# A decode step on one core: the order of narrow attention scores, of their transposes, and of the first and last steps

## The chip, the cores and the metric

The kernel runs on one core of one Trainium2 chip. The metric is device time in microseconds (us) of one execution. Before the change the median of three runs is 603.91 us (602.45 to 604.02).

The engines are named as in the profile: PE is the tensor engine (its weight loads are listed apart, as PEld), DVE the vector engine, ACT the scalar engine with its function tables, POOL the general engine, and SP the one that issues most of the transfers.

## The reference

One decoder layer and a final norm, for a prompt of 256 tokens and for 8 sequences of 4 new tokens each with 2048 cached tokens:

```
h = rms_norm(x, g);  z = h @ w_in          # one projection for all head groups
y_a = silu(c_g) * short_conv(...)          # gated convolution
k_cmp = compress(kv_all[k], ...)           # 64 cached keys pooled to one
s = q @ k_cmp;  p = softmax(s)             # compressed scores, 32 blocks
blocks = top_k(sum of p over heads, forced blocks)
o_sel = softmax(q_rot @ k_sel[blocks]) @ v_sel[blocks]
o_win = softmax(q_rot @ k_win) @ v_win     # the last 512 keys
y_b = silu(n_g) * (g0*o_cmp + g1*o_sel + g2*o_win)
y_m = silu(m_g) * attend(m_q, mem_k, mem_v)   # 256 memory tokens
y = rms_norm(x + concat(y_a, y_b, y_m) @ w_out, final_g)
```

`rms_norm` divides by the root of the mean square. The memory keys and values of the prompt come from `rms_norm(mem_prompt) @ w_mem_kv`. The new cache rows are returned as well.

## The kernel before, in words

The main stream of PE is the projection. Tokens (288 of them, prompt and sample together) are the moving columns, and the weights come as 128 x 1024 halves, each of eight 128 x 128 tiles. Both sides are split into a high and a low part, so that a half is 24 products: high by high, high by low, low by high. `w_load` brings a half from memory, `w_hi` (ACT) rounds it, and `w_lo` (DVE) makes the rest, `wl`. The first four halves, for the memory keys of the prompt, are multiplied without a split, by `first_tiles` (line 290): two output tiles `zf` of 16 steps (k tiles) each. Its input is scaled by `m_scale` (four DVE operations of 256 elements and one ACT copy, the high part) and `m_low` makes the low part for the tiles that follow. Two tiles of PSUM take the outputs in turn; `mem_tile` evicts each on ACT.

All other work is spread between these products by a planner that runs when the program is built. Small generators yield between their steps. `chunk` (line 162) moves the plan's clock `now` by one and lets each waiting generator take a step; it is called twice for a half, every 12 products. The planner keeps its own estimates of the engines' clocks in `at`: `matmul` (line 113) adds 0.2 us for each change between products with 32 weight columns and others, `until` yields while PE's clock is behind another engine's. The result is one fixed order of instructions on each engine.

The work for the 8 sequences goes in two halves of four sequences (`hf` 0 and 1). `stage_stream` (line 821) takes staged pieces of the caches in a fixed order. Cached keys are multiplied with the queries by `scores` (line 494): 16 products of 32 weight columns, four bands of 32 rows that share one PSUM tile, which ACT copies into 512 columns of the score tile `S`. The cached values (`values`, line 625) and the sample's memory keys and values (`memk_use`, `memv_use`) are visits of the same narrow form. `dec_cmp` (line 443) projects the pooled keys and values, multiplies the queries with the compressed keys (tile `sc`, eight products of 32 columns, narrow as well), takes their softmax, and turns the 16 largest blocks into an additive mask `madd`. `dec_softmax` (line 554) adds the mask, 64 keys a block, and takes the softmax. `weights` (line 614) transposes four times 128 columns of `S`, into `pv`: a value tile holds four successive keys in each partition, so transpose n takes every fourth column, n, n + 4, and so on.

`rsqrt` (line 200) makes 1/root in steps: a `Sqrt` on ACT, a reciprocal on DVE, one Newton step on DVE. It is used for the memory tokens and the input rows near the start, and at the end for three groups of rows (two of 128 prompt tokens, one of the sample, called r0, r1 and r2 here). At the end the last 512 output columns are computed with tokens as rows. `squares` sums them, `factors` calls `rsqrt`, `spread_rows` (line 1716) brings the factors of the rows across the partitions with a product (tile `rb`), `scale_tiles` multiplies the 12 column tiles with them, four at a time, and sends them out. `decode_rows` are the sample's products for these columns, 16 steps, and between step `SPREAD_AT` (line 75) and the next stands the spread of r1. `busy` issues products whose result isn't used.

Of the kernel before, what the change touches and what calls it, by code (L numbers as in the profile page):

```python
# [12 lines left out]
AF = mybir.ActivationFunctionType  # L13
ALU = mybir.AluOpType
AX = mybir.AxisListType
# [58 lines left out]
TAIL_BUSY = (4, 6)  # L74
SPREAD_AT = 13
DT = 12
# [4 lines left out]
def decode_step(ctx, tc, xT, xN, xD, xL, fgl, memT, cst, w_in, w_mem, w_out, w_bg, pt, ptv, ckc, ckk, ckv, wk, wv, mk, mv,  # L81
# [59 lines left out]
    vec, act = Timed(nc.vector, VEC, 0.03, 0.0011), Timed(nc.scalar, ACT, 0.16, 0.00083)  # L141

    def behind(i, j):

        at[i] = max(at[i], at[j])
# [48 lines left out]
    def C(name):  # L194
        o, w = _COFF[name]
        return c[:, o:o + w]
# [3 lines left out]
    def rsqrt(r, ssq, rest=None, room=None):  # L200

        v, t = room or (small(3, "yv", 1)[:, :r.shape[1]], small(3, "yt", 1)[:, :r.shape[1]])
        if rest is not None:
            act.activation(r, ssq, AF.Sqrt, scale=1.0 / D, bias=rest[0])
            vec.scalar_tensor_tensor(v, ssq, -0.5 / D, rest[1], op0=ALU.mult, op1=ALU.add)
            vec.reciprocal(r, r)
            vec.scalar_tensor_tensor(t, r, r, v, op0=ALU.mult, op1=ALU.mult)
            vec.scalar_tensor_tensor(r, t, 1.5, r, op0=ALU.add, op1=ALU.mult)
            return
        act.activation(r, ssq, AF.Sqrt, scale=1.0 / D, bias=C("eps"))  # L210
        vec.tensor_scalar(v, ssq, 1.0 / D, EPS, op0=ALU.mult, op1=ALU.add)
        vec.reciprocal(r, r)
        vec.tensor_tensor(t, r, r, op=ALU.mult)
        vec.scalar_tensor_tensor(t, t, -0.5, v, op0=ALU.mult, op1=ALU.mult)
        vec.scalar_tensor_tensor(r, t, 1.5, r, op0=ALU.add, op1=ALU.mult)
# [74 lines left out]
    def first_tiles():  # L290
# [7 lines left out]

        for k0 in (0, 2, 4, 6):
            for i in range(2):  # L300
                part(i, k0, 2)
            if k0 == 2:
                first_loads(0)
                m_scale(8)
                m_low(0)
            elif k0 == 4:
                m_scale(12)
                m_low(4)
            elif k0 == 6:
# [12 lines left out]
        for s in (2, 3):  # L322
            w_hi(s + 2)
            w_lo(s + 1)
            part(s - 2, 8, 4)
            chunk()
            part(s - 2, 12, 4)
            w_load(s + WR)
            first_loads(s)
            nhalf[0] = s + 1  # L330
            yield z[s - 2]
# [111 lines left out]
    def dec_cmp(hf):  # L443
# [12 lines left out]
        act.activation(Vc, t[:, :256], AF.Copy)  # L456
        yield from until(VEC)
        S = env["S", hf]
        s = pss.tile([128, 512], F32, name=f"sc{hf}", tag="s")
# [34 lines left out]
    def scores(hf, o, t, keys):  # L494

        s = pss.tile([128, 512], F32, name=f"sk{hf}", tag="s")
        keys = [keys(x) for x in t]
        for c0 in range(2):
            for g in range(2):
                for b in range(4):  # L500
                    matmul(s[32 * b:32 * b + 32, c0 * 256:c0 * 256 + 256], qcols(0, 4 * hf + b, g), keys[2 * c0 + b // 2](b % 2, g),
                           start=(g == 0), stop=(g == 1), skip_group_check=True)
        act.activation(env["S", hf][:, o:o + 512], s, AF.Copy)

# [23 lines left out]
    def wink_use(hf, t):  # L528
# [17 lines left out]
        vec.tensor_tensor(S[:, C_NW:C_NW + 32], s[:, 32:64], nmask, op=ALU.add)  # L546
        w = S[:, C_NW - 4:C_NW]
        behind(VEC, ACT)
# [5 lines left out]
    def dec_softmax(hf):  # L554
# [4 lines left out]
        for i in range(4):  # L559
            sel = S[:, C_SEL + i * 512:C_SEL + (i + 1) * 512].rearrange("p (n j) -> p n j", j=64)  # L560
            vec.tensor_tensor(sel, sel, env["madd", hf][:, i * 8:i * 8 + 8].unsqueeze(2).to_broadcast([128, 8, 64]), op=ALU.add)
            vec.tensor_reduce(mx[:, i:i + 1], sel, axis=AX.XY, op=ALU.max)
            yield 1
# [50 lines left out]
    def weights(hf, q):  # L614

        o = C_WIN if q == 0 else C_SEL + (q - 1) * 512
        w = env["S", hf][:, o:o + 512]
        parts = w.rearrange("p (r c) -> p c r", c=4)
        t = ptr.tile([128, 512], F32, name=f"pv{hf}", tag="t")
# [5 lines left out]
    def values(hf, i, t):  # L625

        o, PT = env["o"], env["PT", hf, i]
        t = [x.rearrange("p (n c) -> p n c", n=4) for x in t]
# [49 lines left out]
    def memk_use(j, t):  # L678
        if j == 0:
            assert "o" not in env  # L680
            env["o"] = 1
            env["mo"] = pos.tile([128, 512], F32, name="smd", tag="o")
        s = env["mo"]
        for h, x in enumerate(t):
            tv = x.rearrange("p (c s) -> p c s", c=4)
# [35 lines left out]
    def memv_use(j, t):  # L721
        if j == 0:
# [4 lines left out]
            env["mo"] = pos.tile([128, 512], F32, name="omd", tag="o")  # L727
        o = env["mo"]
        PTm = Sm.rearrange("p b s -> p (b s)")
        for k, x in enumerate(t):  # L730
# [181 lines left out]
    nc.gpsimd.memset(z0, 0.0)  # L912
    act.activation(small(1, "mx1"), z0[:, 0:1], AF.Sqrt)
    ps = pss.tile([128, 512], F32, name="zeros", tag="s")
# [690 lines left out]
    def second_pass(n, z):  # L1605
# [10 lines left out]
        if n == DT - 3:  # L1616
            act.activation(small(1, "mx1"), C("eps"), AF.Sqrt)

# [97 lines left out]
    def spread_rows(g, r):  # L1716
        n, k = (128, 128) if g < 2 else (32, 32)
        matmul(rb[:, g * 128:g * 128 + n], r[:k].to_broadcast([k, 128]), ident[:k, :n], start=True, stop=True)

# [58 lines left out]
    matmul(ssq[:, 3:4], sel, sums2[:, 2:3], start=True, stop=True)  # L1778
    scale_tiles(1, 4, 8, nc.sync)
    gains(2)  # L1780
    scale_tiles(1, 8, 12, nc.sync)
    r2 = factors(2, ssq[:, 3:4])
# [139 lines left out]
```

## Time and profile before

| | |
|---|---|
| median of three runs | 603.91 us |
| the profiled execution | 602.7 us |
| its span, first to last instruction | 600.9 us |
| PE busy | 593.2 us, 4827 instructions |
| DVE busy | 457.2 us, 739 instructions |
| ACT busy | 303.5 us, 541 instructions |
| POOL busy | 204.3 us, 281 instructions |
| mean granted PE clock | 0.999 |
| moved by DMA | 190.84 MB |

The lines of the profile that follow name an engine, an operation and the tiles (`out<-in`) with their shape and count. In a timeline the first column is the start in us from the span's start, the second the duration of the group. A group's idle time stands in square brackets, with what ended it. Products are pipelined: one starts before the one ahead of it has ended, so the distance from start to start is what a product costs, and not its duration. Nearly all operations have the line of a helper, so the tiles' names tell them apart.

### The profile page before, as it was taken

The page shows a single profiled execution, that of the slowest core. Times are in us where ns is not written, and L with a number is a line of the kernel's source. Part 1 is how long each engine was busy: PE and PEld are TensorE (multiplying, and loading weights), DVE is VectorE, ACT ScalarE, POOL GpSimd, SP SyncE. Part 2 cuts the span into 40 slices and gives each one's busy share as a digit, 9 for nine tenths or more (in the row PEclk, how much of TensorE's full clock was granted, in tenths as well). Part 3 has the DMA queues.
Part 4 walks back from the last instruction along what each step waited for, and adds up shares of the span by engine and source line. Part 5 has one row for each costly group of instructions (what it writes and reads, how often), then busy time and mean ns, then how long its engine had stood idle before and what let it go on. Part 6 is the DMA issues. An engine that isn't in the chain of part 4 may idle for free.

```text
span 600.9 us, 13265 instructions
## 1 busy us (share of the span) xinstructions
PE 593.2 (99%) x4827; PEld 544.4 (91%) x4827; DVE 457.2 (76%) x739; ACT 303.5 (51%) x541; POOL 204.3 (34%) x281
## 2 busy tenths in 40 slices
PE   8999999999999999999999999999999999999997
PEld 6987999989999999989999899999998998979996
DVE  3999799988596679978897879887768742357665
ACT  4887446444456434434455444555553453435653
POOL 2013554434245333414554544223111334422200
PEclk9999999999999999999999999999999999999999
DMA  8999888999989998987799898898989999979834
GB/s 306 416 429 399 272 306 319 325 306 375 326 269 370 380 415 308 342 327 248 265 331 326 286 368 289 276 339 290 317 311 331 363 333 318 326 253 365 280 143 159
DMA packets 76194, 190.84 MB, mean 318 GB/s; under 512 B 8864, under 2 KB 26432, under 8 KB 75872
## 3 DMA queue, kind: packets, MB, share of 16 engines
q0 software_dynamic: 26016, 100.48, 47.4%
q1 hardware_dynamic: 49104, 88.12, 40.8%
q10 hardware_dynamic: 1008, 1.38, 0.7%
q8 instruction: 38, 0.62, 0.4%
q14 instruction: 28, 0.23, 0.1%
HBM read 184.74 MB, written 13.60 MB: 330 GB/s over the span
## 4 chain that ended last, share of the span: by engine, by line
PE 87%; DVE 7%; DMA 3%; issue 1%; ACT 1%; ACTq 0%; SPq 0%; DVEq 0%
PE z L121 61%; PE zr L121 4%; PE zv L121 4%; PE od L121 3%; PE sk L121 3%; DMA mraw<-memT 2%; DVE pooled L138 2%; PE s L121 2%; DVE wl L138 2%; PE acc L121 2%; PE pv L126 1%; PE pt L126 1%; PE zf L121 1%; DMA st<-ckc 1%; PE om L121 1%
## 5 line engine op out<-in xcount | busy, mean ns | idle before, releaser
L121 PE MATMUL z<-x,wh 128*128 128x288 f32 x1664 | 248.2, 298 | 0.4 <-ACT wh L138 0.4
L121 PEld LDWEIGHTS z<-x,wh 128*128 128x128 f32 x1664 | 227.4, 188 | 7.0 <-issue 4.2
L138 DVE TENSOR_TENSOR wl<-w,wh 128x1024 fp32r<-128x1024 f32 x147 | 181.7, 1239 | 63.7 <-PE z L121 33.2
L138 ACT ACTIVATE wh<-w 128x1024 fp32r<-128x1024 f32 x148 | 154.3, 1052 | 20.0 <-PE z L121 13.1
L121 PE MATMUL z<-x,wl 128*128 128x288 f32 x832 | 127.0, 295 | 0.6 <-DVE wl L138 0.6
L121 PEld LDWEIGHTS z<-x,wl 128*128 128x128 f32 x832 | 115.3, 188 | 1.5 <-DVE wl L138 1.4
L415 POOL TENSOR_TENSOR st<-st,cst 128x512 f32<-128x512 f32 x56 | 62.3, 1112 | 109.5 <-issue 55.5
L230 POOL DMA_DIRECT2D w<-w_in x104 | 58.4, 562 | 111.9 <-DVE wl L138 79.3
L138 DVE TENSOR_REDUCE pooled<-st 128x16 f32<-128x1024 f32 x56 | 67.7, 1210 | 2.2 <-POOL st L415 2.1
L138 DVE TENSOR_TENSOR st<-st,cst 128x512 f32<-128x512 f32 x56 | 39.1, 697 | 8.0 <-DMA st<-ckc 7.9
L230 POOL DMA_DIRECT2D w<-w_out x32 | 17.6, 551 | 67.3 <-DVE wl L138 42.1
L642 POOL DMA_INDIRECT st<-ckv,rows_v x29 | 31.5, 1087 | 22.0 <-PE od L121 13.0
L138 ACT ACTIVATE P<-P,nm 128x128 f32<-128x128 f32 (+1 forms) x32 | 14.2, 444 | 30.3 <-DVE nm L138 30.3
L121 PE MATMUL z<-y,wh 128*128 128x288 f32 x192 | 27.2, 294 | 0.0
L121 PEld LDWEIGHTS z<-y,wh 128*128 128x128 f32 x192 | 26.0, 188 | 0.1
L121 PE MATMUL sk<-st,qz 128*32 128x256 f32 x288 | 19.7, 382 | 0.0
L121 PE MATMUL od<-st,S 128*32 128x256 f32 x288 | 18.9, 382 | 0.0
L138 ACT ACTIVATE se<-z 128x288 f32<-128x288 f32 x16 | 6.4, 401 | 22.0 <-PE z L121 22.0
L121 PE MATMUL zf<-mixed,w 128*128 128x256 f32 x64 | 15.3, 394 | 1.0 <-DVE mixed L138 0.7
L121 PEld LDWEIGHTS zf<-mixed,w 128*128 128x128 f32 x64 | 12.0, 194 | 4.7 <-DVE mixed L138 2.4
L121 PE MATMUL z<-y1b,wh 128*128 128x288 f32 x84 | 15.3, 296 | 0.0
L138 ACT ACTIVATE P<-P,sm 128x128 f32<-128x128 f32 (+1 forms) x32 | 11.9, 444 | 6.4 <-DVE sm L138 6.2
(356 smaller groups left out, 813.2 us busy)
## 6 DMA issues: line engine op xcount, KB each, us to landing
w<-w_in POOLq DMA_DIRECT2D x104, 512.0 KB, 6.3
st<-ckc SPq DMA_DIRECT2D x112, 256.0 KB, 5.9
w<-w_out POOLq DMA_DIRECT2D x32, 512.0 KB, 6.2
st<-ckk SPq DMA_DIRECT2D x112, 128.0 KB, 4.9
w<-w_mem SPq DMA_DIRECT2D x12, 512.0 KB, 7.4
o_wk<-wk POOLq DMA_DIRECT2D x8, 512.0 KB, 7.5
o_wv<-wv POOLq DMA_DIRECT2D x8, 512.0 KB, 7.3
qk<-ckc SPq DMA_DIRECT2D x16, 256.0 KB, 6.2
```

The source lines that it names most:

```text
L121: nc.tensor.matmul(out, a, b, **kw)
L126: nc.tensor.transpose(out, a, b)
L138: return getattr(self.engine, name)(*args, **kw)
L230: (nc.gpsimd if s >= ON_SYNC else nc.sync).dma_start(raws[s], wsrc[s])
L415: done.append(eng.tensor_tensor(tm[:, :, kv], tm[:, :, kv], acmp[:, kv].unsqueeze(1).unsqueeze(1).to_broadcast([128, 2, 4, 64]), op=ALU.mu ...
L642: nc.gpsimd.indirect_dma_start(t, None, ckv, bass.IndirectOffsetOnAxis(ap=rows_v[:, j * 4 + b:j * 4 + b + 1], axis=0))
```

## The change

- `dec_cmp` waits, for up to six chunks, until a narrow visit has been planned in the same chunk, and puts the compressed scores behind it (`beside`). The narrow visits (`scores`, `values`, `memk_use`, `memv_use`) note the chunk in `narrow`.
- `scores` writes its 512 columns as four groups of 128: key 4r + c of the piece goes to column 128c + r. `weights` then transposes adjacent columns. The mask of the window, the addition of `madd` and the maximum follow the new order.
- `rsqrt` uses one ACT function for 1/root, without the reciprocal; the two calls that prepare ACT's table use it as well.
- `first_tiles` takes the two tiles in turn up to k tile 12, and two of its side steps are reordered.
- At the end: `SPREAD_AT` 11 for 13; the spread of the sample's factors uses all 128 rows; one `scale_tiles` goes ahead of `gains(2)`.

```diff
-SPREAD_AT = 13
+SPREAD_AT = 11
...
+    narrow = [-1]
+    def beside(n):
+        for _ in range(n):
+            if narrow[0] == now[0]:
+                return
+            yield 1
...
-            act.activation(r, ssq, AF.Sqrt, scale=1.0 / D, bias=rest[0])
+            act.activation(r, ssq, AF.Abs_reciprocal_sqrt, scale=1.0 / D, bias=rest[0])
             vec.scalar_tensor_tensor(v, ssq, -0.5 / D, rest[1], op0=ALU.mult, op1=ALU.add)
-            vec.reciprocal(r, r)
...
-        act.activation(r, ssq, AF.Sqrt, scale=1.0 / D, bias=C("eps"))
+        act.activation(r, ssq, AF.Abs_reciprocal_sqrt, scale=1.0 / D, bias=C("eps"))
         vec.tensor_scalar(v, ssq, 1.0 / D, EPS, op0=ALU.mult, op1=ALU.add)
-        vec.reciprocal(r, r)
...
-        for k0 in (0, 2, 4, 6):
+        for k0 in (0, 2, 4, 6, 8, 10):
             for i in range(2):
                 part(i, k0, 2)
             if k0 == 2:
+                m_low(0)
+                m_scale(8)
                 first_loads(0)
-                m_scale(8)
-                m_low(0)
             elif k0 == 4:
+                m_low(4)
                 m_scale(12)
-                m_low(4)
...
             w_lo(s + 1)
-            part(s - 2, 8, 4)
-            chunk()
             part(s - 2, 12, 4)
...
         act.activation(Vc, t[:, :256], AF.Copy)
         yield from until(VEC)
+        yield from beside(6)
         S = env["S", hf]
...
     def scores(hf, o, t, keys):
+        narrow[0] = now[0]
...
-        act.activation(env["S", hf][:, o:o + 512], s, AF.Copy)
+        act.activation(env["S", hf][:, o:o + 512].rearrange("p (c r) -> p c r", c=4), s.rearrange("p (r c) -> p c r", c=4), AF.Copy)
...
-        w = S[:, C_NW - 4:C_NW]
+        w = S[:, C_WIN:C_NW].rearrange("p (c r) -> p c r", c=4)[:, :, 127]
...
-            sel = S[:, C_SEL + i * 512:C_SEL + (i + 1) * 512].rearrange("p (n j) -> p n j", j=64)
-            vec.tensor_tensor(sel, sel, env["madd", hf][:, i * 8:i * 8 + 8].unsqueeze(2).to_broadcast([128, 8, 64]), op=ALU.add)
-            vec.tensor_reduce(mx[:, i:i + 1], sel, axis=AX.XY, op=ALU.max)
+            sel = S[:, C_SEL + i * 512:C_SEL + (i + 1) * 512].rearrange("p (c n j) -> p c n j", c=4, j=16)
+            madd = env["madd", hf][:, i * 8:i * 8 + 8].unsqueeze(1).unsqueeze(3).to_broadcast([128, 4, 8, 16])
+            vec.tensor_tensor(sel, sel, madd, op=ALU.add)
+            vec.tensor_reduce(mx[:, i:i + 1], sel.rearrange("p c n j -> p (c n j)"), axis=AX.X, op=ALU.max)
...
-        parts = w.rearrange("p (r c) -> p c r", c=4)
+        parts = w.rearrange("p (c r) -> p c r", c=4)
...
     def values(hf, i, t):
+        narrow[0] = now[0]
...
-    act.activation(small(1, "mx1"), z0[:, 0:1], AF.Sqrt)
+    unit = small(1, "mx1")
+    nc.gpsimd.memset(unit, 1.0)
+    act.activation(unit, unit, AF.Abs_reciprocal_sqrt)
...
-            act.activation(small(1, "mx1"), C("eps"), AF.Sqrt)
+            act.activation(small(1, "mx1"), C("eps"), AF.Abs_reciprocal_sqrt)
...
-        n, k = (128, 128) if g < 2 else (32, 32)
-        matmul(rb[:, g * 128:g * 128 + n], r[:k].to_broadcast([k, 128]), ident[:k, :n], start=True, stop=True)
+        n = 128 if g < 2 else 32
+        matmul(rb[:, g * 128:g * 128 + n], r.to_broadcast([128, 128]), ident[:, :n], start=True, stop=True)
...
     scale_tiles(1, 4, 8, nc.sync)
+    scale_tiles(1, 8, 12, nc.sync)
     gains(2)
-    scale_tiles(1, 8, 12, nc.sync)
     r2 = factors(2, ssq[:, 3:4])
```

More of the change, by code (lines that the diff above doesn't have):

```diff
@@ L683, in memk_use @@
         s = env["mo"]
+        narrow[0] = now[0]
         for h, x in enumerate(t):
@@ L728, in memv_use @@
         o = env["mo"]
+        narrow[0] = now[0]
         PTm = Sm.rearrange("p b s -> p (b s)")
```

## The prediction

> **What bounds the kernel now.** I read the page first, then the chain of waits, then the timeline of TensorE (PE) and of VectorE (DVE) at each place that the diff touches.
>
> ```profile
> span 600.9 us, 13265 instructions
> PE 593.2 (99%) x4827; PEld 544.4 (91%) x4827; DVE 457.2 (76%) x739; ACT 303.5 (51%) x541; POOL 204.3 (34%) x281
> PE 87%; DVE 7%; DMA 3%; issue 1%; ACT 1%; ACTq 0%; SPq 0%; DVEq 0%
> ```
>
> PE is busy for 593.2 of the 600.9 us, and 87% of the chain that ends last is PE's own work. A part of the change is therefore worth what it takes out of PE's stream, or out of the few links that are not PE's: the first 20 us, where data arrive, and the last 8 us, where a short serial chain of small operations ends the run. What VectorE or ScalarE (ACT) save elsewhere is worth nothing. The profiled execution took 602.7 us, 1.8 more than its span; the median of the three runs is 603.9, which is 1.2 above it. I work out a difference against the span and apply it to the median. About 0.3%, or 1.8 us, is what a measurement of this kernel can tell from no change.
>
> **Part 1: scores of compressed keys beside a visit of staged pieces.** The four-band products (32 columns of weights each) leave the usual 128 x 128 form of the products, and going in and out costs time.
>
> ```profile
> 203.25 0.33 PE L121 MATMUL sc<-kcT,qz 128*32 128x32 f32 x16
> 203.51 0.80 PE L121 MATMUL z<-x,wh 128*128 128x288 f32 x4
> 204.15 1.21 PE L121 MATMUL z<-x,wl 128*128 128x288 f32 x8
> 205.29 1.93 PE L121 MATMUL sk<-st,qz 128*32 128x256 f32 x32
> 207.15 1.85 PE L121 MATMUL z<-x,wh 128*128 128x288 f32 x12
> ...
> 214.13 2.27 PE L121 MATMUL z<-x,wh 128*128 128x288 f32 x16
> 216.24 1.22 PE L121 MATMUL z<-x,wl 128*128 128x288 f32 x8
> ```
>
> The first column is the start. Undisturbed, 16 products take from 214.13 to 216.24, which is 0.132 each. For half 0 the scores `sc` stand alone: 0.26 from 203.25 to the next product at 203.51. The four products behind them take 0.64 (to 204.15) where 4 x 0.132 is 0.53, so leaving costs 0.11. Entering is read at `sk` two lines on: the eight products ahead of it take 1.14 (204.15 to 205.29) instead of 1.06, so 0.08. Alone, `sc` costs 0.26 + 0.11 + 0.08 = 0.45.
>
> ```profile
> 442.55 1.07 PE L121 MATMUL sk<-st,qz 128*32 128x256 f32 x16
> ...
> 444.30 0.31 PE L121 MATMUL sc<-kcT,qz 128*32 128x32 f32 x16
> 444.54 2.25 PE L121 MATMUL z<-x,wh 128*128 128x288 f32 x15
> ```
>
> For half 1 the plan already has `sc` right behind `sk`, so the new wait finds nothing to do there. These rows give the price of being beside: `sk` to `sc` is 1.75 and `sc` to the product 0.24, together 1.99, where `sk` to a product took 1.86 (205.29 to 207.15). So 0.13 instead of 0.45: the change gains **0.32 once**, not twice. In half 0 the next narrow visit is the `sk` one chunk later, so the wait is one chunk of its six. It is a wait of the plan and not of an engine: nothing is queued behind it on PE, but the small DVE and ACT operations that make the block mask come about 4 us later. They are wanted only by the softmax of half 0, which waits for the window keys anyway, and their visit comes only after the products quoted at 214 to 217. At nothing, then; if that cover were gone, the whole half, softmax and values, would move back by a chunk.
>
> **Part 2: cached keys' scores in the order of their transposes.** `scores` now permutes while ACT evicts, so that `weights` reads 128 adjacent elements for each transpose instead of every fourth. The transposes `pv` have a twin with adjacent elements, `scpt`, with the same neighbours (a narrow visit before, a product after).
>
> ```profile
> 284.65 0.75 PE L126 MATMUL pv<-cst,S 128*128 128x128 f32 x4
> 285.15 0.77 PE L121 MATMUL z<-x,wh 128*128 128x288 f32 x4
> ```
> ```profile
> 260.26 0.66 PE L126 MATMUL scpt<-cst,scpT 128*128 128x128 f32 x4
> 260.68 0.77 PE L121 MATMUL z<-x,wh 128*128 128x288 f32 x4
> ```
>
> Four strided transposes hold PE for 0.50, four adjacent ones for 0.42: 0.08 each time. `weights` runs five times for each of two halves, so 10 x 0.08 = **0.8**, all on PE. Two of the ten follow other transposes and may gain less; 8 x 0.08 = 0.64 is the lower end if only the visits' neighbours gain.
>
> ```profile
> L138 ACT ACTIVATE S<-sk 128x512 f32<-128x512 f32 x10 | 6.0, 598 | 17.3 <-PE sk L121 17.3
> L138 ACT ACT_TABLE_LOAD x3 | 3.8, 1283 | 4.6 <-DMA w<-w_mem 4.6
> ```
>
> The price may be at the other end: the ten evictions `S<-sk`, 0.60 each, now read PSUM with a step of four. No row shows a strided read of PSUM by ACT; between 0.60 (no effect) and 1.2 (half speed) I take 0.60, because the number of elements stays. Even 1.2 would mostly stand beside PE work, because ACT splits weights two halves ahead; it would count only for the window keys of half 0, whose eviction starts a long DVE stretch: 0.6 at most. [...] VectorE's additions on the permuted scores keep their number of elements too and lie beside PE's products; without that cover their eight calls would add what their new pattern costs, which no row shows.
>
> **Part 3: the first tiles.** The two tiles now advance in step up to the twelfth k tile, and `m_low` comes ahead of `m_scale` on DVE.
>
> ```profile
> 15.24 5.45 PE L121 MATMUL zf<-mixed,w 128*128 128x256 f32 x24 [0.29 <-DVE mixed L138]
> 20.35 0.81 PE L121 MATMUL z<-m0a,wh 128*128 128x256 f32 x4
> ```
> ```profile
> 11.00 0.62 DVE L138 TENSOR_SCALAR mixed<-mraw,mraw 128x256 f32<-128x256 f32 x2 [1.66 <-DMA mraw<-memT]
> 14.83 1.27 DVE L138 TENSOR_SCALAR mixed<-mraw,mraw 128x256 f32<-128x256 f32 x4
> 16.01 1.22 DVE L138 TENSOR_TENSOR m<-mixed,m0a 128x1024 fp32r<-128x1024 f32 x1
> 20.86 1.22 DVE L138 TENSOR_TENSOR wl<-w,wh 128x1024 fp32r<-128x1024 f32 x1
> ```
> ```profile
> 19.93 0.36 ACT L138 ACTIVATE mixed<-zf 128x256 f32<-128x256 f32 x1
> ```
> ```profile
> 7.47 0.33 SPq L230 DMA_DIRECT2D w<-w_mem  x1
> ```
> ```profile
> DMA to landing us min/median/max: 6.7/6.7/6.7
> ```
>
> At 15.24 PE had waited for the scaled twelfth tile, with 24 of 64 instructions left. In the new order 16 of those 24 need it, so this wait goes. What is late next? First the second tile's late weights, now needed eight instructions earlier: issued at 7.47, landed 6.7 later (the last line is that transfer's), at 14.2, so a shorter wait takes the place of the old one, and PE would end the tiles about 0.2 earlier. Then the eviction: the next product reuses the first tile's PSUM, whose eviction by ACT runs from 19.93 to 20.29, and the product started at 20.35. ACT's queue ahead of that eviction is unchanged, and begins with data that land at the same time. So the next product still starts at 20.35, and the reorder itself gains 0.
>
> ```profile
> 21.70 0.28 PE L121 MATMUL z<-m,wh 128*128 128x256 f32 x1
> 21.82 0.28 PE L121 MATMUL z<-m0a,wh 128*128 128x256 f32 x1
> 22.13 0.39 PE L121 MATMUL z<-m0a,wl 128*128 128x256 f32 x1
> ```
>
> The DVE part does gain. The correction half `wl`, which ran from 20.86 to 22.08, is first used at 22.13, 0.31 after the product before where the step is 0.12: a wait of 0.19. In the new order the first `m_low` (1.22 each, as at 16.01) runs in the hole of 1.66 before 11.00, the second takes its old place before 14.83, and everything behind 16.01 moves up by about 1.2, `wl` with it. **0.2** on PE, between 0 and 0.2. The moved `first_loads(0)` passes no other transfer in SP's queue. The sixth buffer's reload follows the first tile's end, now some 1.3 later, and stands behind transfers already queued: at nothing, and up to 1.3 of landing time if they were done.
>
> **Part 4: the end.** The reciprocal goes, the spread of r1 stands two rows earlier, and the last scaling of the second row group goes ahead of `gains(2)`.
>
> ```profile
> 590.36 3.20 PE zd L121 x106
> ```
> ```profile
> 592.72 0.16 DVE L138 SCALAR_TENSOR_TENSOR yr<-yt,yr 128x1 f32<-128x1 f32 x1
> 594.01 1.28 DVE L138 TENSOR_TENSOR yo<-ysum,rb 128x512 f32<-128x512 f32 x2 [1.14 <-PE rb L121]
> 595.23 0.29 DVE L138 TENSOR_TENSOR yod<-zd,st 128x128 f32<-128x128 f32 x1
> 595.44 0.68 DVE L138 TENSOR_TENSOR yo<-ysum,rb 128x512 f32<-128x512 f32 x1
> 596.29 0.22 DVE L138 SCALAR_TENSOR_TENSOR yt<-yr,yv 128x1 f32<-128x1 f32 x1
> ```
> ```profile
> 593.49 0.49 PE L121 MATMUL rb<-cst,yr 128*128 128x128 f32 x2
> 596.76 0.40 PE L121 MATMUL rb<-cst,yr 32*128 32x32 f32 x2 [0.22 <-DVE yr L138]
> ```
> ```profile
> 595.68 0.26 ACT L138 ACTIVATE yr<-ssqy,yrest 128x1 f32<-128x1 f32 x1 [0.47 <-PE ssqy L121]
> ```
>
> Two decode rows are 16 instructions; 106 take 3.20, so 0.48. r1 is ready at 592.88 (592.72 + 0.16), so the spread `rb` can stand at 593.01 instead of 593.49 without a wait. DVE's scalings start 0.48 earlier, at 593.53: two take 1.22 (594.01 to 595.23), a third 0.61, `gains` 0.21 (595.23 to 595.44), so DVE is free at 595.57. The last factor's root leaves ACT at 595.94 (595.68 + 0.26), the step `yt` can follow at about 595.97 instead of 596.29, since no reciprocal stands between: 0.32. From there to the end everything hangs on that link: `rb` at 596.76, scaling, the last transfer. PE had waited 0.22 before that `rb`; behind it stands the filler work, so between 0.2 and 0.32. I take **0.3**. The last `rb` with 128 rows instead of 32 lies between its own 0.40 and the 0.49 of the full-size `rb` at 593.49: 0 to 0.09, taken as 0, since it keeps its 32 columns. The third scaling's transfer leaves earlier and isn't the last one; `gains(2)` behind it is wanted only by the scaling after r2. The shorter chain of r0 is hidden by PE's rows of the second group: 0.
>
> The other two reciprocals (memory and x rows, near 30 us) stand beside PE work and count nothing; the extra memset at the start is queued on POOL behind the one that PE waits for.
>
> **Sum:** 0.32 + 0.8 + 0.2 + 0.3 = 1.62, so 602.7 becomes 601.1 and the median 603.9 becomes 602.3.
>
> **Rivals.** *The plan shifts for the better.* The planner adds the cost of each change of form to its PE clock; with half 0's taken out, that clock runs 0.4 earlier from 203 us on, and some later visits move by a chunk. If two or three separate small visits happen to meet others, each saves up to 0.32: 2.6 in all, 601.3. *It shifts for the worse:* two or three visits part company, or one DVE wait of that size appears: 0.7 in all, 603.2. The profile can't say which; there are many visits, and the shift is a quarter of a chunk. *The strided read isn't what makes `pv` longer* (the change does not do what it says): 0.8 less, 603.1. Against it: twin and `pv` differ in nothing else that the rows show.
>
> *The reciprocal root needs a table of its own that has no Square* — the slower side. In the trace each of three table loads takes 1.283 us, and three are too few for a load between square sum and root at the end: the old root shares its table with Square, which speaks for Square being common. If the new root did not, a load would stand between each of the three square sums and its root. r0's would hold PE's second group of rows by up to 1.28. r1 would come at 594.16 instead of 592.88 and PE would wait 1.15 at the spread (593.01); r2's 1.28 is wholly on the last link. That is 3.7, against the gain of 1.6: 606.0. It decides as soon as one load stands between a square sum and its root. [...]
>
> **How the numbers follow.** Forecast 0.56, better plan 0.20, worse plan 0.14, strided read 0.06, table 0.04. With the lower ends of parts 2 to 4 the forecast reaches 602.7, with a slow eviction 603.3; on the other side r0's chain and overlaps that I left out may add some tenths, and medians of a few runs scatter, so its own range is 601.6 to 603.2, and 0.21 of its 0.56 lies beyond 1.8 us of gain. Faster: 0.21 + 0.20 = 0.41. Slower: the table's 0.04 and 0.04 of the worse plan: 0.08. Within: 0.51. The likeliest time is 602.3. The range reaches from the better plan with a low median (the three runs lie 1.6 apart) at 600.7 to the worse plan with a high one at 604.4; the table case is left out.
>
> **What would show it.** Right: `sc` of half 0 straight behind an `sk`, with no product between; `pv` to the next product 0.42; three table loads; the first `wl` product without a gap, but the first product still near 20.3 with ACT's eviction before it; DVE's last `yt` right behind ACT's root, and the span 1.6 shorter. Wrong: a fourth table load; `S<-sk` clearly above 0.60; new PE waits for DVE or for weights between 205 and 530; or a first product well ahead of 20.3, which would mean that the eviction did not bound it.

## The result, and the profile after

The changed kernel takes 611.0 us (median of six runs, 609.43 to 612.36) where the kernel before took 603.8 beside it: a ratio of 1.0122, 95% interval 1.0107 to 1.0138. It is 7.2 us slower; I had forecast 1.6 faster. The ratios here and below leave out three executions far off the others (645 us of the kernel before, 2058 of `warm4`, 3316 of `only_layout`). From the page of the changed kernel's profiled execution:

```profile
span 607.7 us, 13255 instructions
...
PE 595.2 (98%) x4827; PEld 545.7 (90%) x4827; DVE 458.9 (76%) x734; ACT 303.0 (50%) x541; POOL 209.5 (34%) x282
...
PE 84%; DVE 10%; issue 2%; ACT 2%; DMA 1%; SPq 0%; DVEq 0%; ACTq 0%
```

PE has the same 4827 instructions and 2.0 us more busy time, so that most of the 6.8 us that the span grew is idle. In the chain, VectorE's share rose from 7% to 10%. The list of what PE waited for (total, times, longest) names it:

```profile
PE z L121 <- DVE se L138: 1.4, 1, 1.4
PE z L121 <- ACT y L138: 1.3, 1, 1.3
...
PE ot L126 <- DVE odr L138: 1.0, 1, 1.0
PE vc L121 <- DVE PT L138: 1.0, 1, 1.0
...
PE sc L121 <- ACT S L138: 0.4, 1, 0.4
...
PE acc L121 <- DVE pcT L138: 0.4, 1, 0.4
PE z L121 <- ACT y1b L138: 0.3, 1, 0.3
```

None of these seven is in the list of before. They sum to 5.8 us, and all but `acc` hang on one chain of work, that of the second half of the sequences (`vc`, `sc`, softmax, `od`, `ot`), or on what it meets. Its timeline on PE:

```profile
443.70 1.10 PE L126 MATMUL pt<-cst,P 128*128 128x128 f32 x8
445.78 0.71 PE L121 MATMUL vc<-cst,pooled 128*128 128x128 f32 x4 [0.98 <-DVE PT L138]
...
452.55 1.93 PE L121 MATMUL sk<-st,qz 128*32 128x256 f32 x32
454.30 0.50 PE L121 MATMUL sn<-qk,qz 128*32 128x32 f32 x32
455.23 0.33 PE L121 MATMUL sc<-kcT,qz 128*32 128x32 f32 x16 [0.42 <-ACT S L138]
...
482.49 1.20 PE L121 MATMUL z<-y1a,wh 128*128 128x288 f32 x7 [1.37 <-DVE se L138]
484.62 1.06 PE L121 MATMUL z<-y1b,wh 128*128 128x288 f32 x5 [0.27 <-ACT y1b L138]
...
542.37 1.93 PE L121 MATMUL od<-st,S 128*32 128x256 f32 x32
545.34 0.30 PE L126 MATMUL ot<-cst,odr 128*128 128x128 f32 x1 [1.03 <-DVE odr L138]
546.91 1.25 PE L121 MATMUL z<-y,wh 128*128 128x288 f32 x5 [1.27 <-ACT y L138]
```

`vc` waits 0.98 for a PSUM tile: the prompt's transposes `pt`, planned just ahead of it now, have taken both, and VectorE has yet to read one. In the kernel before, `sc` of half 1 stood at 444.30, behind the `sk` at 442.55. Now it has missed that visit and stands at 455.23, behind the next `sk` and behind `sn`; it wants a PSUM tile that both have just filled, and waits 0.42 for ACT to evict the first. The softmax that follows comes later too, and falls on the time when the output of the memory heads (`odr<-omd`) is wanted. VectorE's timeline there:

```profile
476.37 0.69 DVE L138 TENSOR_REDUCE mx<-S 128x1 f32<-128x512 f32 x1
476.97 1.22 DVE L138 TENSOR_TENSOR wl<-w,wh 128x1024 fp32r<-128x1024 f32 x1
...
479.61 1.13 DVE L138 SCALAR_TENSOR_TENSOR odr<-omd,cst,odr 128x128 f32<-128x128 f32 x3
480.85 1.22 DVE L138 TENSOR_TENSOR wl<-w,wh 128x1024 fp32r<-128x1024 f32 x1
481.99 0.45 DVE L138 SCALAR_TENSOR_TENSOR se<-se,z 128x288 f32<-128x288 f32 x1
```

VectorE has no gap between these, and the maxima of the softmax stand ahead of the output; `se` ends at 482.44, and PE, which had waited 1.37 for it, goes on at 482.49. The last link is the dearest. Before, the last values visit stood well ahead of the second pass of the output projection:

```profile
529.85 1.93 PE L121 MATMUL od<-st,S 128*32 128x256 f32 x32
...
534.62 0.27 PE L126 MATMUL ot<-cst,odr 128*128 128x128 f32 x1
...
540.31 0.95 PE L121 MATMUL z<-y,wh 128*128 128x288 f32 x6
```

10.5 us lay between the start of `od` and the first product that needs its result, filled with row products. Now nothing is left between them: `od` at 542.37, then a serial chain over VectorE, PE (`ot`), ACT, VectorE and ACT, and the pass begins at 546.91. From 542.37 to there 4.54 pass: 1.93 of `od`, 0.30 of `ot` and 2.30 of the two waits. These waits cost more than their idle time, because the first products behind them step more slowly: 0.24 once behind 482.49, 0.26 and 0.24 behind 484.62, 0.46 and 0.24 behind 546.91, where the rest step at 0.13.

The waits' 5.8, less some 1.2 that the parts gain (below), are 4.6 of the 6.8 by which the span grew. Of the other 2.2, the slow steps behind those three waits make 0.8, and the first tiles end 0.5 later in this profile; what is left is in no single row and stays open.

What the prediction said of the four parts is there, all the same. `sc` of half 0 stands in its narrow visit, and the transposes are shorter (timelines of PE). Behind them stand the group of their weight loads, and the groups of the eviction and of the table loads:

```profile
207.42 0.29 PE L121 MATMUL sc<-kcT,qz 128*32 128x32 f32 x4
207.64 1.85 PE L121 MATMUL z<-x,wh 128*128 128x288 f32 x12
...
287.25 0.66 PE L126 MATMUL pv<-cst,S 128*128 128x128 f32 x4
287.67 1.56 PE L121 MATMUL z<-x,wh 128*128 128x288 f32 x10
```

```profile
L126 PEld LDWEIGHTS pv<-cst,S 128*128 128x128 f32 x40 | 4.3, 140 | 3.3 <-issue 2.9 <-PE od L121 0.4
...
L138 ACT ACTIVATE S<-sk 128x512 f32<-128x512 f32 x10 | 6.0, 598 | 21.5 <-PE sk L121 21.5
...
L138 ACT ACT_TABLE_LOAD x3 | 3.8, 1283 | 4.3 <-DMA w<-w_mem 4.3
```

In the kernel before the weight loads of `pv` stood so:

```profile
L126 PEld LDWEIGHTS pv<-cst,S 128*128 128x128 f32 x40 | 5.6, 210 | 3.3 <-issue 2.9 <-PE od L121 0.4
```

`pv` to the next product takes 0.42 instead of 0.50; its weight loads take 140 ns each instead of 210; the eviction of `sk` keeps its 598 ns; there are three table loads.

### The profile page after: what moved, and what is told of

It is laid out like the page before. It is cut to its first block, busy times and chain, and to the rows that moved or that the text cites. A ratio compares the mean times of both kernels' runs of the same rounds, so it can differ in the third digit from the quotient of the medians.

```text
span 607.7 us, 13255 instructions
## 1 busy us (share of the span) xinstructions
PE 595.2 (98%) x4827; PEld 545.7 (90%) x4827; DVE 458.9 (76%) x734; ACT 303.0 (50%) x541; POOL 209.5 (34%) x282
## 4 chain that ended last, share of the span: by engine, by line
PE 84%; DVE 10%; issue 2%; ACT 2%; DMA 1%; SPq 0%; DVEq 0%; ACTq 0%
PE z L121 57%; PE zv L121 4%; PE zr L121 4%; PE od L121 3%; PE sk L121 3%; PE zf L121 3%; DVE pooled L138 2%; DVE wl L138 2%; PE s L121 2%; PE acc L121 1%; PE pv L126 1%; DVE st L138 1%; PE pt L126 1%; PE zd L121 1%; DVE S L138 1%
## 5 line engine op out<-in xcount | busy, mean ns | idle before, releaser
L420 POOL TENSOR_TENSOR st<-st,cst 128x512 f32<-128x512 f32 x56 | 63.9, 1141 | 101.0 <-DVE st L138 58.1
L651 POOL DMA_INDIRECT st<-ckv,rows_v x29 | 36.6, 1261 | 24.4 <-PE od L121 14.4
L138 ACT ACTIVATE S<-pv 128x512 f32<-128x512 f32 x10 | 6.0, 599 | 31.3 <-PE pv L126 25.5
L121 PEld LDWEIGHTS zf<-mixed,w 128*128 128x128 f32 x64 | 13.6, 217 | 3.8 <-DVE mixed L138 1.7
L121 PE MATMUL zf<-mixed,w 128*128 128x256 f32 x64 | 16.9, 429 | 0.1
L138 ACT ACTIVATE S<-sk 128x512 f32<-128x512 f32 x10 | 6.0, 598 | 21.5 <-PE sk L121 21.5
```

The source lines that it names most:

```text
L121: nc.tensor.matmul(out, a, b, **kw)
L138: return getattr(self.engine, name)(*args, **kw)
L420: done.append(eng.tensor_tensor(tm[:, :, kv], tm[:, :, kv], acmp[:, kv].unsqueeze(1).unsqueeze(1).to_broadcast([128, 2, 4, 64]), op=ALU.mu ...
L651: nc.gpsimd.indirect_dma_start(t, None, ckv, bass.IndirectOffsetOnAxis(ap=rows_v[:, j * 4 + b:j * 4 + b + 1], axis=0))
```

## The experiments

**Theory A, the plan:** no instruction became dearer. The wait in `dec_cmp` makes the planner's PE clock run 0.4 earlier behind `sc` of half 0 (two changes of form less), generators step in other chunks, and work lands where PE must wait. **Theory B, the layout or the first tiles:** a strided eviction, four-dimensional patterns on VectorE, or the new order at the start cost the time. **Theory C, the delay:** it is the scores of half 0 one chunk later that hold the rest up. Under A there is a second question: does the moved prompt attention cost the time (A2), or the place of half 1's chain (A1)?

The plan is fixed when the program is built, so the place of each piece can be counted in the order of PE's instructions: in chunks of 12 products of the main stream, the second pass beginning at 252 in all of them. Ratios are against runs of the kernel before on the same chip.

| kernel | `vc`, half 1 | `sc`, half 1 | its softmax ends (`pe`) | last `od` | median us | ratio (95%) |
|---|---|---|---|---|---|---|
| before | 206 | 208 | 228 | 249 | 603.2 to 603.8 | 1 |
| changed | 209 | 212 | 233 | 252 | 611.0 | 1.0122 (1.0107 to 1.0138) |
| all_but_beside | 206 | 208 | 228 | 249 | 602.85 | 0.9987 (0.9974 to 1.0001) |
| clock_back | 206 | 208 | 228 | 249 | 602.15 | 0.9984 (0.9974 to 0.9993) |
| clock_alone | 209 | 211 | 230 | 250 | 607.42 | 1.0071 (1.0051 to 1.0090) |
| half0_only | 209 | 211 | 230 | 250 | 607.50 | 1.0075 (1.0042 to 1.0108) |
| half1_late | 206 | 212 | 233 | 252 | 606.65 | 1.0049 (1.0036 to 1.0062) |
| clock_08 | 207 | 208 | 226 | 248 | 608.01 | 1.0069 (1.0053 to 1.0085) |
| prompt_late | 208 | 209 | 228 | 249 | 602.59 | 0.9989 (0.9975 to 1.0003) |
| last_prompt_late | 209 | 212 | 233 | 252 | 610.71 | 1.0124 (1.0107 to 1.0142) |

**Is it part 1, and is it the wait or the clock?** Four kernels. `all_but_beside` leaves the wait out:

```diff
-        yield from beside(6)
```

> All of the change but the wait for a narrow visit (part 1). Theory A, the plan: the whole loss comes from part 1, because with it the order of PE's instructions differs from before in some 300 places and without it only in the first tiles and the last rows. Then this kernel has the order of before and gains 0.8 (adjacent transposes) and 0.3 (tail), less at most 0.5 lost in the first 21 us: 602.7 to 603.3 us, ratio to before 0.998 to 0.999. Theory B, the data layout: the eviction with a step of four, the additions with four-dimensional patterns or the new order of the first tiles cost more than they save; then this kernel keeps most of the loss, 608 or more.

Measured 602.85, ratio 0.9987: the loss is gone with the wait. Theory B falls. `clock_back` is the whole change with the clock mended:

```diff
                                  start=(g == 0), stop=(g == 1), skip_group_check=True)
+        if hf == 0:
+            at[0] += 0.4
         mx, nm, sm = small(1, "mx1"), small(1, "nm1"), small(1, "sm1")
```

> The whole change, and one line more: behind the scores of half 0 the planner's PE clock is set forward by 0.4, the two changes of form that it no longer counts. Every other visit then falls into the chunk that it had before. Theory A: the wait itself is harmless and worth the 0.32 that I worked out, the clock does the damage: 0.3 below the kernel without the wait, 602.4 to 603.0, ratio 0.997 to 0.998. Theory C, the delay: the scores of half 0 one chunk later (and the importance and block mask behind them) are what delays the rest; then the clock changes nothing and this kernel stands near 611, as the changed kernel does. Theory B: near 611 as well.

Measured 602.15, a little under the range expected, ratio 0.9984, interval 0.9974 to 0.9993: this is faster than the kernel before and than the changed one, and it has the wait. Theory C falls: half 0's `sc` is one chunk later here too. Part 1's own saving shows in its timeline:

```profile
205.03 1.93 PE L121 MATMUL sk<-st,qz 128*32 128x256 f32 x32
206.78 0.31 PE L121 MATMUL sc<-kcT,qz 128*32 128x32 f32 x16
207.01 1.85 PE L121 MATMUL z<-x,wh 128*128 128x288 f32 x12
```

From `sk` to the product behind `sc` are 1.98; the prediction had read 1.99 from half 1. Product for product, this kernel is 0.20 behind the kernel before ahead of that place (196.7) and 0.13 ahead of it behind it (216.8): 0.33 saved, where I had 0.32. `clock_alone` has the clock's error and no wait:

```diff
-        yield from beside(6)
...
+        if hf == 0:
+            at[0] -= 0.4
```

> The whole change without the wait, but with the planner's PE clock set back by 0.4 behind the scores of half 0, which stand alone where they stood before. No instruction is saved. Theory A: later visits move as in the changed kernel, half 1's scores of compressed keys come 3 chunks later instead of 4, its last values visit stands 2 chunks ahead of the second pass instead of at its first product, and PE has less to wait for there: slower than before by 2 to 6 us, 606 to 610. Theory C: with no delay of half 0's scores there is no loss, 602.7 to 603.3. Theory B: near 611, like every kernel with the layout.

Measured 607.42, ratio 1.0071. A number in the planner, with no instruction changed by it but the order, costs 4.6 us against `all_but_beside`. And `half0_only` leaves half 1's wait out:

```diff
-        yield from beside(6)
+        if not hf:
+            yield from beside(6)
```

> The change with the wait in half 0 alone; half 1's scores go at once. This tests my step that for half 1 the wait finds nothing to do. Theory A, with two parts: the clock moves half 1's chain 3 chunks back, and the wait then holds its scores one chunk more and its softmax until it meets the memory heads' output on VectorE. Without the wait the last values visit is 2 chunks ahead of the second pass: 606 to 610, clearly below the changed kernel's 611, and within 0.5 of the kernel in which only the clock is moved. If half 1's wait costs nothing, 611.

Measured 607.50 (one of its seven executions, at a mean clock of 0.947, took 613.3), as with the clock alone, and by the ratios 2.8 below the changed kernel. So half 1's wait, which I had called idle, does something as soon as the clock has moved its chain: one chunk more at `sc`, two at the last `od`, which then has no cover left.

**Prompt work or half 1's chain?** `half1_late` has the order of before and holds only half 1's `sc`, by four chunks:

```diff
-        yield from beside(6)
+        if hf:
+            yield 4
+        else:
+            yield from beside(6)
```

> The kernel with the clock set back, and half 1's scores of compressed keys held four chunks: half 1's importance, softmax and values then stand in exactly the chunks of the changed kernel (last values visit at the second pass's first product), while everything else (prompt keys, prompt scores, half 1's pooled keys) keeps the order of before. Theory A1, the place of half 1's chain: it carries most of the loss. From the waits of the changed kernel that hang on this chain (0.42 at sc, 1.37 and 0.27 behind the memory heads' output, 1.03 and 1.27 at the second pass: 4.4) the time is 606.5 to 608.5, the waits at 482 and at the start of the second pass come back, those at 239, 317 and for vc do not. Theory A2, the moved prompt work does it: 602 to 603.5.

Measured 606.65, just inside A1's range; by the ratios 3.9 more than `clock_back`. Its timeline on PE has three of the waits again, and one at the memory heads' output, at `otm` instead of `se`:

```profile
452.84 0.33 PE L121 MATMUL sc<-kcT,qz 128*32 128x32 f32 x16 [0.42 <-ACT S L138]
...
477.40 0.33 PE L126 MATMUL otm<-cst,odr 128*128 128x128 f32 x1 [0.72 <-DVE odr L138]
...
541.24 0.30 PE L126 MATMUL ot<-cst,odr 128*128 128x128 f32 x1 [0.98 <-DVE odr L138]
542.81 4.15 PE L121 MATMUL z<-y,wh 128*128 128x288 f32 x16 [1.27 <-ACT y L138]
```

The counterpart, `prompt_late`, moves the prompt's attention (its last group by 7 chunks, 10 in the changed kernel) and leaves half 1's softmax and values where they were:

```diff
+                if (2, 0, 1, 5)[2 * g + tt]:
+                    yield (2, 0, 1, 5)[2 * g + tt]
                 yield from prompt_nsa(g, tt)
```

> The counterpart of the kernel with half 1's chain held (606.65). Clock set back as in the kernel that stood at 602.15, and the prompt's attention held by 2, 0, 1 and 5 chunks ahead of its four groups: the last group's transposes then stand 7 chunks later (the changed kernel: 10), half 1's pooled keys 2 later (there 3), but half 1's scores only 1 later and its softmax and values in the chunks of before. Theory A1, the place of half 1's chain decides: 602 to 603.5. Theory A2, the moved prompt work has a price of its own, the other half of the changed kernel's loss: 605 to 607.

Measured 602.59, ratio 0.9989: no loss, although its profile has a wait of 1.04 behind the memory heads' output (`y1b`). A2 falls as far as this kernel goes: the prompt's last group may stand 7 chunks late at no price that the median shows. It matters through what it pushes and what it meets. That is `last_prompt_late`: the same edit with (0, 0, 0, 9), all else as in `clock_back`, and the planner itself puts half 1's whole chain where the changed kernel has it:

> Clock set back as well, and only the prompt's last group held, by 9 chunks. The planner then puts half 1's pooled keys, scores, softmax and values into exactly the chunks of the changed kernel; all ahead of the last group (scores of half 0 included) keeps the order of before. If the changed kernel's loss is made by what the plan does from the last prompt group on, the waits for vc (0.98), sc (0.42), behind the memory heads' output (1.6 together) and at the second pass (1.03 and 1.27) all come back: 609.5 to 611. If the earlier moves at 239 and 317 matter, 608 or less.

Measured 610.71, ratio 1.0124: the changed kernel's loss in full. From its timeline on PE:

```profile
446.26 0.71 PE L121 MATMUL vc<-cst,pooled 128*128 128x128 f32 x4 [0.97 <-DVE PT L138]
...
482.78 1.19 PE L121 MATMUL z<-y1a,wh 128*128 128x288 f32 x7 [1.17 <-DVE se L138]
485.10 1.05 PE L121 MATMUL z<-y1b,wh 128*128 128x288 f32 x5 [0.48 <-ACT y1b L138]
...
547.34 2.71 PE L121 MATMUL z<-y,wh 128*128 128x288 f32 x16 [1.27 <-ACT y L138]
```

So what the plan does from the prompt's last group on carries the loss: the place of half 1's chain, and at `vc` the prompt's transposes that now stand just ahead of it. By the ratios 4.5 lie between this kernel and `half1_late`. The rows show 0.97 of it at `vc` and 0.93 more at the memory heads' output (1.17 + 0.48 against 0.72); where the rest is stays open, since the two profiles differ by 1.1 at the first tiles as well, by chance. Product for product the two drift apart by 3.1 between 388 and 489 us, and in its profile `half1_late` loses 1.5 of that again at half clock (below).

**Is later worse, or merely other?** `clock_08` is `clock_alone` with 0.8 for 0.4; half 1's softmax and values then stand earlier than before (its `vc` one chunk later):

> The whole change without the wait, the planner's PE clock set back by 0.8 behind the scores of half 0 instead of 0.4. Prompt work moves as much as with 0.4, but half 1's chain comes out EARLIER than before (last values visit 4 chunks ahead of the second pass, before it was 3). Theory A1: no loss, 602 to 604. If an earlier clock is bad in itself, or the moved prompt work, 606 or more.

Measured 608.01: that expectation falls. (The prompt's transposes move by 0 to 2 chunks here, with 0.4 by up to 10, so this kernel says little of them.) The place of the chain decides, but earlier isn't better as such. PE's timeline shows why:

```profile
482.75 0.30 PE L126 MATMUL otm<-cst,odr 128*128 128x128 f32 x1 [1.94 <-DVE odr L138]
484.08 1.59 PE L121 MATMUL z<-y1b,wh 128*128 128x288 f32 x5 [1.03 <-ACT y1b L138]
```

The softmax, now two chunks early, ends just ahead of the memory heads' output instead of behind it, and both use the one tile `odr`. The softmax has it from 477.36 until PE reads it at 480.00 (`pe`, with `pv` right behind), and VectorE stands idle ahead of the output:

```profile
481.10 0.35 DVE L138 TENSOR_SCALAR odr<-omd,cst 128x128 f32<-128x128 f32 x1 [3.45 <-PE pv L126]
```

PE waits 1.94 for it, and then 1.03 for ACT. Something else costs as much. The view by windows (the column behind POOL is the granted clock of PE):

```profile
core 0: us, PE busy (x) PEld busy (x) DVE busy (x) ACT busy (x) POOL busy (x), PEclk, DMA share, GB/s
484.00:487.00 3.00, 2.92 (x12) 2.92 (x13) 1.05 (x3) 0.55 (x2) 0.00 (x0) 0.50 1.03 418
```

The granted clock is 0.50. Taken by single microseconds it is 0.50 from 483.0 to 489.8, some 6.8 us, which begin behind the wait of 1.94 and hold the one of 1.03; in the rest PE does half of what it could: about 3 lost, as much as by the two waits. `half1_late` has it too, behind its waits of 0.98 and 1.27 at the start of the second pass:

```profile
543.00:546.50 3.50, 3.44 (x14) 3.23 (x14) 2.32 (x3) 0.71 (x1) 0.56 (x1) 0.51 0.86 357
```

There the 16 products from 542.81 take 3.99 (to 546.80) where 16 undisturbed ones take 2.11 in the kernel before: 1.9 lost behind 2.25 of idle time. `clock_alone` has a stretch of 3.4 us at half clock too. The profiled execution of the changed kernel has none but in its last 0.4 us, so its loss does not need one. Of its six executions the two at a mean clock of 1.000 took 609.4 and 610.8, the four at 0.995 to 0.997 took 609.5 to 612.4.

**The other parts alone.** `only_layout`, `only_first` and `only_ends` are the kernel before with part 2, part 3 and part 4 (root and tail), each as in the change's diff.

> The kernel before with the cached keys' scores in the order of their transposes alone. My prediction: 0.8 gained (0.64 at least), the eviction unchanged at 0.60: ratio 0.9985 to 0.999. Rival, the eviction and VectorE's new patterns cost something: 0.9995 or more.

Measured 602.80, ratio 0.9990 (0.9978 to 1.0001): 0.6 to 0.9 gained, by ratio and medians, where I said 0.8. The interval just touches 1; the rows are clearer: every `pv` costs 0.09 to 0.10 less behind a narrow visit, eight times, and 0.05 behind other transposes, twice: 0.8. But 0.2 is given back at once. In its timeline on PE:

```profile
478.32 1.18 PE L121 MATMUL z<-y1a,wh 128*128 128x288 f32 x7 [0.25 <-DVE se L138]
```

PE comes 0.45 earlier to the memory heads' output, and VectorE doesn't. This wait is not in before.

> The kernel before with the first tiles' new order alone. My prediction: 0.2 gained, the first product still at 20.35. The four new profiles so far have it at 20.0 to 21.5, in the order of how long PE's products step at 0.43 us instead of 0.22 at the start (until 5.8, 8.6, 9.8, 10.4), and the kernel before has a short slow stretch (until 5.8) in its profile. Theory D: that stretch differs from execution to execution, in before as well, and has nothing to do with the change; with a short one the new order gains 0.3 to 0.5, with a long one the first product is at 20.7 to 21.5 where before would be later still. The median then shows a gain of 0.1 to 0.6: ratio 0.999 to 1.000. Rival: the new order itself makes PE start slow, then 0.5 to 1 lost: ratio 1.001 or more.

Measured 603.42, ratio 1.0007 (0.9996 to 1.0018): no gain to be seen. The first product is at 19.99 in its profile, 0.36 earlier than before. ACT's eviction bounds it all the same: it ends at 19.94 here, at 20.30 before, because ACT's work ahead of it stands earlier. And the product's place differs from execution to execution by more than that. Two profiles of kernels with the same first tiles, `half0_only` first, then `all_but_beside`:

```profile
4.51 15.64 PE L121 MATMUL zf<-mixed,w 128*128 128x256 f32 x64
20.03 0.74 PE L121 MATMUL z<-m0a,wh 128*128 128x256 f32 x4
```

```profile
4.63 17.25 PE L121 MATMUL zf<-mixed,w 128*128 128x256 f32 x64 [0.23 <-DVE mixed L138]
21.53 0.70 PE L121 MATMUL z<-m0a,wh 128*128 128x256 f32 x3
```

The difference of 1.5 lies in the rate of PE's first products: they step at 0.43 until 5.7 in the one and until 10.4 in the other, and at 0.22 from there on. By the clock grants that the traces list, the stretch ends between 4.6 and 10.6 in the 14 profiles, with the old order (5.8, 8.7 and 4.6) as with the new (5.1 to 10.6). Theory D's stretch is there; its gain of 0.1 to 0.6 is not in the median. Three profiles of the old order can't say whether the new one makes the stretch longer, and the interval doesn't exclude the rival's 0.5.

> The kernel before with part 4 alone: reciprocal root for root and reciprocal, the spread two rows earlier, the third scaling ahead of the last factors. My prediction: 0.3 gained (0.2 to 0.32), ratio 0.9995, which a median can hardly show; in the profile three table loads, the last step of the factor right behind the root, and from the last row product to the end of the span 0.3 less than before.

Measured 602.95, ratio 1.0001 (0.9987 to 1.0014). In its profile the span ends 10.77 behind the start of the last row product, in before 10.89: 0.12 gained, not 0.3.

> The kernel with the clock set back, with four instead of three products of zeros ahead of the first tiles: they then reach to 5.3 us and cover PE's idle time of 0.1 to 0.7 before the first tiles and most of their first wait. Theory D1: PE steps at 0.43 us until it has been busy for some us without a hole, so the hole ahead of the first tiles is what prolongs the slow stretch in some executions (until 8.5 to 10.4); without it the stretch ends by 8 in every execution and the median falls by 0.3 to 0.8 below 602.15. Theory D2: its length has nothing to do with the hole: no gain, or 0.3 lost by starting the first tiles later.

`WARM` 4 for 3, on top of `clock_back`. Measured 601.77, ratio 0.9979 (0.9968 to 0.9990); 0.4 under `clock_back`, with intervals that overlap. In the one profile the half-rate steps end at 7.2. It fits D1 and does not show it.

## Why the prediction was wrong, point by point

**Part 1 is the step that failed**, in two sentences. For half 0 I let the wait of a chunk cost nothing ("At nothing, then"), since the mask is wanted late. That holds (`clock_back`), but the cost was looked for on the engines, and it arose in the planner. For half 1 I wrote: "the new wait finds nothing to do there". I had read its place from the trace of before, as if the plan stood still. With the clock 0.4 early, half 1's chain is 3 chunks late, its `sc` has just missed the `sk`, and the wait holds it for the next.

**The rival was named and mis-sized.** "It shifts for the worse" had the mechanism: plan, visits, a VectorE wait. Its price (0.7, from "two or three visits part company, or one DVE wait of that size") and its chance (0.14) rested on "the shift is a quarter of a chunk". That is the wrong measure. A generator that misses its chunk loses a whole one, its followers wait for visits that are 4 to 11 chunks apart (half 1's `sk`), and the next bottleneck is not 0.3 but an engine's chain: 1.4, 1.0, 1.0, 1.3. Built with 0.1 for 0.4 (and not run), `clock_alone` has half 1's chain in the same chunks. I had also said that the profile can't tell which way it goes; it could tell what is at stake, because before had only 10.5 us of cover from the last `od` to the second pass, and a softmax on VectorE just ahead of the memory heads' output.

**What held.** With the plan kept, the four parts give 602.15. That this is so near the forecast of 602.3 is luck: the kernel before ran at 603.3 beside it and not at 603.9, and by the ratio the parts gain 1.0 (0.4 to 1.6), where I forecast 1.6. Part 2 is right in size (0.8) and in both of its reasons: the weight loads of `pv` fell from 210 to 140 ns, and the eviction, now with a step of four in its read of PSUM, kept its 598; VectorE's additions on the permuted scores kept their price as well (683 ns each before, 685 in `clock_back`). Of its 0.8, PE gives 0.2 back at once, waiting for VectorE at the memory heads' output. Part 1's saving in half 0 is 0.33 for 0.32. The table rival did not come: three loads, the last at 580.66 in the changed kernel's trace, and none between the square sums and roots from 593.76 to 602.88, so the table of the new root has the squares too. These runs show Square beside both roots and say nothing of other tables.

**Part 3** was right in what bounds the first product, and wrong in a premise: that ACT's queue ahead of the eviction "begins with data that land at the same time". In nine of the 14 profiles, of both orders, the product starts 0.05 or 0.06 behind the end of that eviction (20.35 behind 20.30 before, 19.99 behind 19.94 in `only_first`), but this end lies anywhere between 19.65 and 20.89; in the other five, which come to full rate at 8.7 us or later, PE itself is late. So "the next product still starts at 20.35" fails, though a product well ahead of 20.3 did not mean what I said it would. The wait at the correction half did go: its step is 0.12 in all profiles of the new order, 0.24 to 0.32 with the old. In the median that gain can't be told from nothing. **Part 4** was mis-sized: 0.12 for 0.3. VectorE's last steps in the changed kernel:

```profile
602.91 0.16 DVE L138 SCALAR_TENSOR_TENSOR yv<-ssqy,yrest 128x1 f32<-128x1 f32 x1 [0.31 <-ACT yr L138]
603.11 0.22 DVE L138 SCALAR_TENSOR_TENSOR yt<-yr,yv 128x1 f32<-128x1 f32 x1
```

I let `yt` follow the root at once. `yv` stands ahead of it, and it too waits for the root's end, as it had before (596.04 behind a root that ended at 595.94): only the reciprocal's place was to be had.

## What to carry to other kernels

Where a planner orders the work, an edit that changes its clock changes everything behind it: compare the order of instructions ahead of the times, and if the old order was good, keep its clock (here two lines, worth 8 us). Read from the profile which chains have little cover before the point where all must be done, and which blocks nearly meet on one engine; they say what a shift can cost, and it is not in proportion to the shift. In three of these profiles PE ran at half clock for 3.4 or 6.8 us behind waits of 1.56 to 2.25 us, which cost nearly as much again (1.9 behind 2.25 in `half1_late`); in others, behind waits as long, its clock stayed full.

## What the runs showed of the hardware

- **PE's clock fell to half behind some short holes, for 3.4 or 6.8 us.** Behind 2.25 of idle time in two pieces (`half1_late`) and behind 1.56 (`clock_alone`) PE ran at a granted clock of 0.50 for 3.4 us, behind 1.94 for 6.8 with 1.03 of idle time inside (`clock_08`), and not at all behind waits as long in others (1.03 and 1.27 in the changed kernel, 0.98 and 1.27 in `last_prompt_late`, 1.56 in `half0_only`). The traces list the clock grants: the full one lasts 593.92 us in the kernel before and 597.33 in the changed kernel, 174 and 175 times 3.413, and the stretches at half clock above are one or two such steps long. In the 3.41 us ahead of them PE had stood idle, with short gaps, for 2.25, 1.62 and 1.94. Counted in steps of 3.413 from the changed kernel's first full grant (9.92), its waits of 1.03 and 1.27 lie on both sides of a step's end (545.81), with 1.21 of idle time in the step ahead of it and 1.16 in the one behind. That may be why its clock stayed full; it is not shown, and three cases are few for a limit.
- **PE ran at half rate at the start, and for how long differed from execution to execution:** until 4.6 to 10.6 us in the 14 profiles. The views print a granted clock of 1.00 there, because a trace lists no grant ahead of the first full one; that one (5.75 before, 9.92 in the changed kernel) stands where PE's step from start to start falls to 0.22, in the changed kernel from 0.43.
- **Adjacent or strided weights:** 140 ns (changed kernel) against 210 (before) for a load of 128 x 128 of `pv`, and 0.09 us less for four transposes (`only_layout`). The eviction `S<-sk` by ACT, which reads PSUM with a step of four in the changed kernel, takes the same 598 ns as the adjacent one before.
